# The weights of three of seven up-projection products, moved by 64 bytes inside longer ring buffers

## The chip, the cores and the metric

The kernel runs on one core of a Trainium2 chip. The metric is the device time of one execution in microseconds (us); the number compared is the median of several runs. The profiled execution is one further run, and all rows of the profile come from it.

## What is computed

One layer of a hybrid decoder trunk on 512 tokens with 2048 channels, in float32: a norm, a combined input projection, three groups of mixing heads, an output projection, a gated feed-forward part and a last norm. The reference, cut:

```python
def reference(x, norm1_w, w_in, ..., final_norm_w):
    for l in range(DEPTH):                                    # DEPTH = 1
        h = rmsnorm(x, norm1_w[l])
        u_pool, q, k, v, z, a, bt, xr, gr = jnp.split(h @ w_in[l], cuts, axis=-1)
        y_pool = pool_mixer(u_pool, ...)
        y_gdn = gated_deltanet(q, k, v, z, a, bt, ...)
        y_lru = rglru_mixer(xr, gr, ...)
        mixed = jnp.concatenate([y_pool, y_gdn, y_lru], axis=-1)
        x = x + mixed @ w_out[l]
        x = x + conv_ffn(rmsnorm(x, norm2_w[l]), ffn_up[l], ffn_conv_w[l], ffn_down[l])
    return rmsnorm(x, final_norm_w)

def conv_ffn(h, w_up, conv_w, w_down):
    gate, val = jnp.split(h @ w_up, 2, axis=-1)               # 2048 -> 2 x 6144
    gate = causal_dwconv(gate, conv_w)
    return (jax.nn.gelu(gate) * val) @ w_down                 # 6144 -> 2048
```

## The kernel before

**Products.** Every large product is made of three matmuls on TensorE (PE). Both operands are split into a high and a low part of a reduced float32 format (fp32r): ScalarE (ACT) casts the high part, VectorE (DVE) subtracts it to get the low one, and PE adds hi x hi, hi x low and low x hi into one PSUM bank. The weights are the stationary operand, tiles of 128 x 128 out of a buffer of 128 x 1024, and are loaded anew for each matmul; the tokens are the moving operand. PE and the DMA queue of SyncE (SP) run in the order in which the code is written. In the first part DVE, ACT and GpSimd (POOL) are ordered by the compiler's scheduler, from the up projection on also by the code.

**Stages.** `in_phase` makes 40 units of the input projection, with the heads' work put between them as coroutines (`gdn_gates`, `gdn_front`, `gdn_pair`, `lru_front` and others); then come the output projection, the up projection (class `UpProjection`), the down projection and the last norm.

**The weights' ring.** A weight block is loaded into a `raw` buffer and split into `hi` and `lo`. There are four buffers of each (`NW`), used in turn through the whole kernel, of 4096 bytes a partition: `prep` at L180 for the input and output projections, `split` at L1165 for the up projection, `w_split` at L972 for the down projection.

**The up projection.** It is computed by a scheme with seven products in place of eight (L1123 and following). Weights and tokens are cut in two; for each of the 48 column groups j seven combinations of weight blocks are multiplied with seven forms of the tokens. Three forms are plain blocks (`BLOCKS`: a11, a12, a22), four are sums of blocks (`SUMS`: s1 to s4). A product (`product`, L1180) has 8 steps of three matmuls with 256 moving columns. `ACT_FORM` says which form each product takes:

```python
    ACT_FORM = {"b22": "s4", "b11": "a11", "t3": "s3", "t1": "s1", "t2": "s2", "b21": "a12", "t4": "a22"}
```

A slot is one product; a column group starts seven slots after the one before, so that each stretch of seven slots (a round) holds one of each kind. The weights' combinations are made in place: after a split, POOL issues a DMA that adds the next block into the same `raw` buffer (L1178). Blocks are loaded 7 slots ahead (`LEAD`) and split 3 slots ahead (`LAG`).

**Where the tiles lie.** A tile's place in a partition follows from the pools' order and sizes. The parameters take 1220 bytes, the constants 2048, and what follows lies in steps of 2048 and 4096 bytes. In the built program all `hi` and `lo` buffers and all tiles of the pool `acts` begin 96 bytes into a block of 128 bytes. In `acts` are the split tokens of all projections, the plain blocks (`fa`, `fb`), and the sums' tiles for p = 6 and 7 (`split_sums`, L824: the branch after `p < HK - 2`). The sums' tiles for p = 0 to 5 are in the pool `ffn` and begin 32 bytes into a block of 128. The index p is also the product's step. In the trace the names are `fs` for sums, `fa` and `fb` for plain blocks, `hi_b`, `hi_t`, `lo_b`, `lo_t` for the up projection's weights, and `ps_x`, `ps_y`, `ps_z` for its PSUM banks; the bank does not tell the form, the moving operand's name does.

**Gates and constants.** `cst` in the pool `const` holds four 128 x 128 constants: identity, upper triangle, mask and ones. `softplus` (L138) is used twice in the input phase, for the recurrent block's constants (`spl`, in `lru_consts`) and for the decay gates (`spg`, in `gdn_gates`), on four small scratch tiles each in the pool `g1`. Two short matmuls `ps_g` (L460, L461) take its result `g`; in PE's order the transposes of k and q and what follows of the first heads stand right behind them.

Of the kernel before, what the change touches and what calls it, by code (L numbers as in the profile page):

```python
# [8 lines left out]
F32 = mybir.dt.float32  # L9
F32R = mybir.dt.float32r  # L10
# [8 lines left out]
P = 128  # L19
# [11 lines left out]
NW = 4  # L31
# [4 lines left out]
COL = {}  # L36
# [31 lines left out]
DOWN_GAP = 1.2  # L68
ND = 4
NWARM = 14  # L70
# [9 lines left out]
class Body:  # L80
# [3 lines left out]
    def __init__(self, tc, io):  # L84
        self.tc, self.nc, self.io = tc, tc.nc, io
        self.now, self.cos, self.polling = 0.0, [], False


# [48 lines left out]

    def softplus(self, pool, out, x, n, tag, sign=1.0):  # L138

        nc = self.nc  # L140
        ab = pool.tile([P, n], F32, tag=f"{tag}a", name=f"{tag}_abs")
        u = pool.tile([P, n], F32, tag=f"{tag}u", name=f"{tag}_u")
        s = pool.tile([P, n], F32, tag=f"{tag}s", name=f"{tag}_s")
        z = pool.tile([P, n], F32, tag=f"{tag}z", name=f"{tag}_z")
        nc.vector.tensor_scalar(ab, x, -1.0, None, op0=ALU.mult)
        nc.vector.tensor_tensor(out=u, in0=ab, in1=x, op=ALU.min)
        nc.scalar.activation(u, u, AF.Exp)
        nc.vector.tensor_scalar(s, u, 2.0, None, op0=ALU.add)
        nc.vector.reciprocal(s, s)
        nc.vector.tensor_tensor(out=s, in0=s, in1=u, op=ALU.mult)  # L150
        nc.vector.tensor_tensor(out=z, in0=s, in1=s, op=ALU.mult)
        nc.vector.memset(u, 1.0 / 17.0)
        for k in (15, 13, 11, 9, 7, 5, 3, 1):
            nc.vector.tensor_tensor(out=u, in0=u, in1=z, op=ALU.mult)
            nc.vector.tensor_scalar(u, u, 1.0 / k, None, op0=ALU.add)
        nc.vector.tensor_tensor(out=u, in0=u, in1=s, op=ALU.mult)
        nc.vector.tensor_scalar(ab, x, sign, 0.0, op0=ALU.mult, op1=ALU.max)
        nc.vector.scalar_tensor_tensor(out=out, in0=u, scalar=2.0, in1=ab, op0=ALU.mult, op1=ALU.add)
# [20 lines left out]

    def prep(self, src, name, pre="w"):  # L180

        nc = self.nc
        raw = self.wp.tile([P, 1024], F32, tag="raw", name=f"raw_{name}", bufs=3)
        nc.sync.dma_start(out=raw, in_=src)
        pool, n = (self.wp, NW) if pre == "w" else (self.wd, ND)
        hi = pool.tile([P, 1024], F32R, tag=pre + "hi", name=f"hi_{name}", bufs=n)
        lo = pool.tile([P, 1024], F32R, tag=pre + "lo", name=f"lo_{name}", bufs=n)
        nc.scalar.copy(out=hi, in_=raw)  # L188
        nc.vector.tensor_tensor(out=lo, in0=raw, in1=hi.bitcast(F32), op=ALU.subtract)  # L189
        return hi, lo  # L190
# [53 lines left out]
    def run(self):  # L244
        tc, nc, io = self.tc, self.nc, self.io
        with ExitStack() as ctx:
# [9 lines left out]
            self.prmt = cp.tile([P, NPRM], F32, name="prmt")  # L256
            cst = cp.tile([P, 4, P], F32, name="cst")
            self.ident, self.upper, self.mask, self.ones = (cst[:, i, :] for i in range(4))
            self.cst = cst
            self.in_phase()  # L260
# [16 lines left out]
    def in_phase(self):  # L277
        tc, nc, io = self.tc, self.nc, self.io
        with ExitStack() as ctx:
# [20 lines left out]

            n1 = g1.tile([P, KT], F32, name="n1")

            warm = self.tmp("warm")
# [25 lines left out]
            for kt in range(KT):  # L329
# [5 lines left out]
                if kt == 12:  # L335
                    nc.sync.dma_start(out=self.cst, in_=io["cst"])
                    nc.sync.dma_start(out=self.prmt, in_=io["prm"])
# [91 lines left out]
    def gdn_gates(self, ssum, psab):  # L429
# [24 lines left out]
        nc.scalar.activation(ea, hb[:, 0:1, :], AF.Exp)  # L454
        self.softplus(g1, f2(g), f2(x), n, "spg")
        nc.vector.scalar_tensor_tensor(out=g, in0=g, scalar=-1.0, in1=ea.broadcast_to([P, NC, H]),
# [243 lines left out]
    def lru_consts(self):  # L700
        nc, g1 = self.nc, self.g1
        n = NB
        sp = g1.tile([P, n], F32, name="lsp")
        self.softplus(g1, sp, self.prmt[:, COL["lam"]:COL["lam"] + n], n, "spl", sign=-1.0)
        self.sc, self.nsc = g1.tile([P, n], F32, name="lsc"), g1.tile([P, n], F32, name="lnsc")
        nc.vector.tensor_scalar(self.sc, sp, -8.0, None, op0=ALU.mult)
        nc.vector.tensor_scalar(self.nsc, sp, 8.0, None, op0=ALU.mult)
# [77 lines left out]
    def out_phase(self):  # L785
        tc, nc, io = self.tc, self.nc, self.io
        with ExitStack() as ctx:
# [184 lines left out]
            def w_split(c, k):  # L972
                hi, lo = (self.wp.tile([P, 1024], F32R, tag=t, name=f"{t}_d{c}_{k}", bufs=NW) for t in ("whi", "wlo"))
                self.parts(raws.pop((c, k)), hi, lo)
                wd.setdefault(c, []).append((hi, lo))
# [147 lines left out]
class UpProjection:  # L1123
# [41 lines left out]
    def split(self, n):  # L1165

        nc, wp = self.nc, self.b.wp
        while self.n_split < min(n, len(self.slots)):
            _, j, f = self.slots[self.n_split]
            self.n_split += 1  # L1170
            raw = self.raw[j, self.CHAIN[f][0]]
            hi = wp.tile([P, 1024], F32R, tag="whi", name=f"hi_{f}_{j}", bufs=NW)
            lo = wp.tile([P, 1024], F32R, tag="wlo", name=f"lo_{f}_{j}", bufs=NW)
            nc.scalar.copy(out=hi, in_=raw)  # L1174
# [85 lines left out]
def _layout(inputs):  # L1260
# [28 lines left out]
    up = i[None, :] >= i[:, None]  # L1289
    r["cst"] = c(np.stack([np.eye(P), up, np.where(up, 0.0, -1e30), np.ones((P, P))]).astype(np.float32)  # L1290
                 .transpose(1, 0, 2))
# [23 lines left out]
```

## Time and profile before

| | us |
|---|---|
| median of 3 runs | 2236.95 |
| range of the runs | 2236.02 to 2238.54 |
| the profiled execution's own time | 2237.1 |
| its span, first to last instruction | 2235.3 |
| first 105 us of it: PE busy | 99.2 |
| input phase and output projection, 105 to 751 us: PE busy | 633.2 |
| up projection, 775 to 1691 us: PE busy | 914.5 |
| down projection, 1702 to 2210 us: PE busy | 508.0 |
| end, 2210 to 2235 us: PE busy | 11.8 |

The up projection's first products run from 740 us on. Rows that begin with a window A:B give its length, then each engine's busy time and number of instructions (PE, PE's weight loads, DVE, ACT, POOL; an engine without instructions is left out), the granted TensorE clock as a share of the full one, the DMA engines' busy share, and GB/s. Rows of the chain and the timeline give start and duration. Rows of groups give busy time and mean ns of one, then the engine's idle time before them and what ended it. Matmuls overlap: one begins while the one before it still drains, so the pace of a stream is the distance between starts, not the duration. Rows of waits give total, number and the longest.

### The profile page before, as it was taken

The numbers are of one execution on the slowest core, as the hardware profiler recorded it, in microseconds if no ns is written. First come the engines' busy times: TensorE is split into PE (matmuls) and PEld (weight loads), VectorE is DVE, ScalarE is ACT, GpSimd is POOL, SyncE is SP. The second block draws the span as 40 slices with busy tenths as digits, with TensorE's granted clock in tenths as the row PEclk, the third lists the DMA queues.
The fourth block names the chain that finished last, engine by engine and source line by source line (L and its number), as shares of the span: only waits on it lengthen the run. The fifth ranks groups of instructions, "written<-read, shape, count | busy, mean of one in ns | idle before, by whom it ended". The sixth has DMA issues, their size and how long they took to land.

```text
span 2235.3 us, 35469 instructions
## 1 busy us (share of the span) xinstructions
PE 2199.9 (98%) x13998; PEld 1991.0 (89%) x13998; DVE 1517.4 (68%) x2340; ACT 944.6 (42%) x1371; POOL 437.6 (20%) x531
## 2 busy tenths in 40 slices
PE   9999999999999999999999999999999999999997
PEld 6878878888888999999999999999998888888887
DVE  8756657664544776667676677676667777777776
ACT  6646455433433544444444444444443222222223
POOL 4270730810122111111111111111110000000004
PEclk9999999999999999999999999999999999999998
DMA  6222222223533788888889888888885333333333
GB/s 199 83 95 66 88 85 81 91 86 112 192 123 117 164 209 207 200 203 198 195 204 209 199 202 196 198 204 207 210 197 189 130 120 126 123 113 123 113 127 100
DMA packets 109208, 340.01 MB, mean 152 GB/s; under 512 B 12720, under 2 KB 19120, under 8 KB 109040
## 3 DMA queue, kind: packets, MB, share of 16 engines
q1 hardware_dynamic: 78576, 229.72, 30.1%
q0 software_dynamic: 30464, 108.02, 26.6%
q8 instruction: 110, 1.80, 0.3%
q14 instruction: 58, 0.48, 0.1%
HBM read 314.36 MB, written 23.33 MB: 151 GB/s over the span
## 4 chain that ended last, share of the span: by engine, by line
PE 85%; POOL 5%; DVE 4%; issue 2%; ACT 2%; DMA 2%; SPq 0%; POOLq 0%; ACTq 0%; DVEq 0%
PE ps_y L1193 17%; PE ps_x L1193 12%; PE ps_z L1193 11%; PE ps_d L203 7%; PE ps_d L201 7%; PE ps_d L202 7%; PE ps_u L201 3%; PE ps_u L202 3%; PE ps_u L203 3%; PE ps_o L202 3%; PE ps_o L201 3%; PE ps_o L203 3%; POOL tm L581 2%; POOL tl L583 2%; DVE lo_in L189 1%
## 5 line engine op out<-in xcount | busy, mean ns | idle before, releaser
L1010 DVE TENSOR_TENSOR accd<-accd,ps_d 128x512 f32<-128x512 f32 x368 | 250.0, 685 | 125.1 <-PE ps_d L203 125.0
L201 PE MATMUL ps_d<-gh,whi_d 128*128 128x512 f32 x736 | 286.3, 389 | 0.0
L202 PE MATMUL ps_d<-gl,whi_d 128*128 128x512 f32 x736 | 286.3, 389 | 0.0
L203 PE MATMUL ps_d<-gh,wlo_d 128*128 128x512 f32 x736 | 286.3, 389 | 0.0
L1193 PE MATMUL ps_y<-fs,hi_t 128*128 128x256 f32 x1536 | 269.8, 278 | 1.8 <-DVE e L1219 1.8
L274 ACT CAST whi_d<-raw_d 128x1024 fp32r<-128x1024 f32 x96 | 100.8, 1053 | 371.7 <-PE ps_d L202 345.5
L1175 DVE TENSOR_TENSOR lo_t<-ra,hi_t 128x1024 fp32r<-128x1024 f32 x144 | 176.0, 1223 | 112.9 <-ACT hi_t L1174 112.8
L201 PE MATMUL ps_u<-xh,hi_in 128*128 128x512 f32 x608 | 246.4, 405 | 0.0
L203 PE MATMUL ps_u<-xh,lo_in 128*128 128x512 f32 x608 | 238.7, 393 | 0.0
L202 PE MATMUL ps_u<-xl,hi_in 128*128 128x512 f32 x608 | 238.1, 392 | 0.0
L1178 POOL DMA_DIRECT2D ra<-in_w_up x144 | 126.2, 876 | 556.8 <-DVE lo_t L1175 457.5
L1193 PEld LDWEIGHTS ps_y<-fs,hi_t 128*128 128x128 f32 x1536 | 233.1, 188 | 2.2 <-ACT hi_b L1174 1.7
L1193 PE MATMUL ps_y<-fs,lo_t 128*128 128x256 f32 x768 | 213.1, 278 | 0.0
L1174 ACT CAST hi_t<-ra 128x1024 fp32r<-128x1024 f32 x144 | 151.3, 1051 | 69.8 <-PE ps_y L1193 43.5
L202 PEld LDWEIGHTS ps_d<-gl,whi_d 128*128 128x128 f32 x736 | 138.1, 188 | 28.8
L203 PEld LDWEIGHTS ps_d<-gh,wlo_d 128*128 128x128 f32 x736 | 138.1, 188 | 28.6
L201 PEld LDWEIGHTS ps_d<-gh,whi_d 128*128 128x128 f32 x736 | 138.1, 188 | 28.6
L189 DVE TENSOR_TENSOR lo_in<-raw_in,hi_in 128x1024 fp32r<-128x1024 f32 x80 | 104.4, 1306 | 78.0 <-ACT hi_in L188 77.4
L1193 PEld LDWEIGHTS ps_y<-fs,lo_t 128*128 128x128 f32 x768 | 144.4, 188 | 0.0
L1193 PE MATMUL ps_y<-fb,hi_t 128*128 128x256 f32 x768 | 140.1, 283 | 1.2 <-DVE e L1223 1.2
L1193 PE MATMUL ps_x<-fb,hi_b 128*128 128x256 f32 x768 | 140.1, 283 | 0.0
L1193 PE MATMUL ps_x<-fa,hi_b 128*128 128x256 f32 x768 | 140.0, 283 | 0.0
(357 smaller groups left out, 5104.7 us busy)
## 6 DMA issues: line engine op xcount, KB each, us to landing
ra<-in_w_up POOLq DMA_DIRECT2D x144, 512.0 KB, 7.7
raw_d<-in_w_down SPq DMA_DIRECT2D x96, 512.0 KB, 4.2
raw_in<-in_w_in SPq DMA_DIRECT2D x80, 512.0 KB, 3.7
ra<-in_w_up SPq DMA_DIRECT2D x48, 512.0 KB, 7.0
rc<-in_w_up SPq DMA_DIRECT2D x48, 512.0 KB, 6.5
rb<-in_w_up SPq DMA_DIRECT2D x48, 512.0 KB, 7.2
rb<-in_w_up POOLq DMA_DIRECT2D x48, 512.0 KB, 7.2
raw_o<-in_w_out SPq DMA_DIRECT2D x32, 512.0 KB, 3.7
```

The lines of the kernel that those rows point to most:

```text
L189: nc.vector.tensor_tensor(out=lo, in0=raw, in1=hi.bitcast(F32), op=ALU.subtract)
L201: nc.tensor.matmul(ps, hi[:, sl], a, start=start, stop=False)
L202: nc.tensor.matmul(ps, hi[:, sl], b, start=False, stop=False)
L203: nc.tensor.matmul(ps, lo[:, sl], a, start=False, stop=stop)
L274: self.nc.scalar.copy(out=hi, in_=x)
L581: nc.gpsimd.tensor_tensor(out=t, in0=bc(ll[:, j, j + 1:32], j + 1), in1=tl[:, j:j + 1, 0:j + 1].broadcast_to([32, m, j + 1]), op=ALU.mult)
L583: nc.gpsimd.tensor_tensor(out=tl[:, j + 1:32, 0:j + 1], in0=tl[:, j + 1:32, 0:j + 1], in1=t, op=ALU.subtract)
L1010: nc.vector.tensor_tensor(out=acc[d], in0=acc[d], in1=ps, op=ALU.add)
L1174: nc.scalar.copy(out=hi, in_=raw)
L1175: nc.vector.tensor_tensor(out=lo, in0=raw, in1=hi.bitcast(F32), op=ALU.subtract)
L1178: nc.gpsimd.dma_start(out=raw, in_=self.block(j, self.NEXT[f]), accum_op=ALU.add)
L1193: mm = lambda w, x, s, e: nc.tensor.matmul(ps, w[:, sl], x, start=s, stop=e, skip_group_check=True)
```

## The change

The ring's buffers become 1040 words (4160 bytes) long in place of 1024, one tag for each, taken in turn by a counter; a weight block fills 1024 words of its buffer, from the first word or from the 17th. Because 4160 bytes are 32.5 blocks of 128, the `hi` buffers begin 96 bytes into such a block and the `lo` buffers 32. `weight_parts` chooses the offset (0 or 64 bytes) so that hi and lo lie at 96 for all products but three, and at 32 for the products with plain blocks (b11, b21, t4). To make room, the upper triangle and the mask move into a pool of the input phase (two loads in place of one), and softplus's scratch becomes one tile of the ring of temporaries for each use.

```diff
-    def softplus(self, pool, out, x, n, tag, sign=1.0):
+    def softplus(self, out, x, n, tag, sign=1.0):
...
-        ab = pool.tile([P, n], F32, tag=f"{tag}a", name=f"{tag}_abs")
-        u = pool.tile([P, n], F32, tag=f"{tag}u", name=f"{tag}_u")
-        s = pool.tile([P, n], F32, tag=f"{tag}s", name=f"{tag}_s")
-        z = pool.tile([P, n], F32, tag=f"{tag}z", name=f"{tag}_z")
+        scr = self.tmp(f"{tag}_scratch", [P, 4, n])
+        ab, u, s, z = (scr[:, i, :] for i in range(4))
...
-    def prep(self, src, name, pre="w"):
+    def weight_parts(self, name, other=False):
+        i = self.n_ring % NW
+        self.n_ring += 1
+        t = [self.wp.tile([P, 1040], F32R, tag=f"w{p}{i}", name=f"{p}_{name}", bufs=1) for p in ("hi", "lo")]
+        o = [16 * ((k + other) % 2) for k in range(2)]
+        return [t[k][:, o[k]:o[k] + 1024] for k in range(2)]
+
+    def prep(self, src, name):
...
-        pool, n = (self.wp, NW) if pre == "w" else (self.wd, ND)
-        hi = pool.tile([P, 1024], F32R, tag=pre + "hi", name=f"hi_{name}", bufs=n)
-        lo = pool.tile([P, 1024], F32R, tag=pre + "lo", name=f"lo_{name}", bufs=n)
+        hi, lo = self.weight_parts(name)
...
-            cst = cp.tile([P, 4, P], F32, name="cst")
-            self.ident, self.upper, self.mask, self.ones = (cst[:, i, :] for i in range(4))
-            self.cst = cst
+            self.cst = cp.tile([P, 2, P], F32, name="cst")
+            self.ident, self.ones = (self.cst[:, i, :] for i in range(2))
...
+            cst2 = g1.tile([P, 2, P], F32, name="cst2")
+            self.upper, self.mask = (cst2[:, i, :] for i in range(2))
...
-                    nc.sync.dma_start(out=self.cst, in_=io["cst"])
+                    nc.sync.dma_start(out=self.cst, in_=io["cst"][:, 0:2])
+                    nc.sync.dma_start(out=cst2, in_=io["cst"][:, 2:4])
...
-                hi, lo = (self.wp.tile([P, 1024], F32R, tag=t, name=f"{t}_d{c}_{k}", bufs=NW) for t in ("whi", "wlo"))
+                hi, lo = self.weight_parts(f"d{c}_{k}")
...
-            hi = wp.tile([P, 1024], F32R, tag="whi", name=f"hi_{f}_{j}", bufs=NW)
-            lo = wp.tile([P, 1024], F32R, tag="wlo", name=f"lo_{f}_{j}", bufs=NW)
+            hi, lo = self.b.weight_parts(f"{f}_{j}", other=self.ACT_FORM[f] in BLOCKS)
```

On PE and POOL the instructions stand in the same order as before, over the whole kernel, and from the output projection on so do those of DVE, ACT and SP. The scheduler's order changes on DVE and ACT in the first units of the input projection. DVE around the gates, before: `spg_u` and `spg_abs` are softplus's scratch, `x_q` and `cv_q` the second q head's evacuation and convolution, `lo_in` the low part of the next unit's weights, `g` the gates, `G` their sums out of PSUM.

```order
L413 TENSOR_TENSOR x_q_711<-ps_u_650,rstd1b 128x512
L156 TENSOR_TENSOR spg_u<-spg_u,spg_s 128x24
L158 SCALAR_TENSOR_TENSOR g<-spg_u,spg_abs 128x24
L189 TENSOR_TENSOR lo_in_1_708<-raw_in_1_705,hi_in_1_707 128x1024
L456 SCALAR_TENSOR_TENSOR g<-g,ea 128x24
L425 SCALAR_TENSOR_TENSOR cv_q_713<-x_q_711,prmt,cv_q_713 128x511
L464 COPY G<-ps_g 128x48
```

The same place of the changed kernel, whose line numbers are 7 higher here (L156 and L158 of before are L154 and L156 of the changed kernel, and L189 is L194):

```order
L420 TENSOR_TENSOR x_q_707<-ps_u_646,rstd1b 128x512
L153 TENSOR_SCALAR spg_scratch<-spg_scratch 128x24
L154 TENSOR_TENSOR spg_scratch<-spg_scratch 128x24
L194 TENSOR_TENSOR lo_in_1_704<-raw_in_1_701,hi_in_1_703 128x1024
L156 SCALAR_TENSOR_TENSOR g<-spg_scratch 128x24
L432 SCALAR_TENSOR_TENSOR cv_q_709<-x_q_707,prmt,cv_q_709 128x511
L463 SCALAR_TENSOR_TENSOR g<-g,ea 128x24
L432 SCALAR_TENSOR_TENSOR cv_q_709<-x_q_707,prmt,cv_q_709 128x510
L471 COPY G<-ps_g 128x48
```

The last steps to g have moved behind the low part, and one convolution step of cv_q stands ahead of the last of them.

SP's queue near the end of the first two units, before: `xraw` are the token tiles, `prmt` the parameters, `raw_in` the third unit's weights.

```order
L313 DMA xraw_368<-in_xT 128x512
L336 DMA cst<-in_cst 128x512
L337 DMA prmt<-in_prm 128x305
L313 DMA xraw_387<-in_xT 128x512
L184 DMA raw_in_0_420<-in_w_in 128x1024
```

In the changed kernel, where the upper triangle and the mask have a transfer of their own:

```order
L319 DMA xraw_369<-in_xT 128x512
L342 DMA cst<-in_cst 128x256
L343 DMA cst_101<-in_cst 128x256
L344 DMA prmt<-in_prm 128x305
L319 DMA xraw_389<-in_xT 128x512
L191 DMA raw_in_0_422<-in_w_in 128x1024
```

One issue stands ahead of the parameters, of the last token tile and of the weights that follow.

More of the change, by code (lines that the diff above doesn't have):

```diff
@@ L68 @@
 DOWN_GAP = 1.2
-ND = 4
 NWARM = 14
@@ L86, in __init__ @@
         self.now, self.cos, self.polling = 0.0, [], False
+        self.n_ring = 0
     def spawn(self, gen):
@@ L454, in gdn_gates @@
         nc.scalar.activation(ea, hb[:, 0:1, :], AF.Exp)
-        self.softplus(g1, f2(g), f2(x), n, "spg")
+        self.softplus(f2(g), f2(x), n, "spg")
         nc.vector.scalar_tensor_tensor(out=g, in0=g, scalar=-1.0, in1=ea.broadcast_to([P, NC, H]),
@@ L703, in lru_consts @@
         sp = g1.tile([P, n], F32, name="lsp")
-        self.softplus(g1, sp, self.prmt[:, COL["lam"]:COL["lam"] + n], n, "spl", sign=-1.0)
+        self.softplus(sp, self.prmt[:, COL["lam"]:COL["lam"] + n], n, "spl", sign=-1.0)
         self.sc, self.nsc = g1.tile([P, n], F32, name="lsc"), g1.tile([P, n], F32, name="lnsc")
@@ L1165, in split @@
     def split(self, n):
-        nc, wp = self.nc, self.b.wp
+        nc = self.nc
         while self.n_split < min(n, len(self.slots)):
@@ L1289, in _layout @@
     up = i[None, :] >= i[:, None]
-    r["cst"] = c(np.stack([np.eye(P), up, np.where(up, 0.0, -1e30), np.ones((P, P))]).astype(np.float32)
+    r["cst"] = c(np.stack([np.eye(P), np.ones((P, P)), up, np.where(up, 0.0, -1e30)]).astype(np.float32)
                  .transpose(1, 0, 2))
```

## The prediction

> **What bounds the kernel now.** I read the page's first part and the windows by stage first, then what TensorE (PE) waits for.
>
> ```profile
> PE 2199.9 (98%) x13998; PEld 1991.0 (89%) x13998; DVE 1517.4 (68%) x2340; ACT 944.6 (42%) x1371; POOL 437.6 (20%) x531
> 775.00:1691.00 916.00, 914.50 (x7805) 914.15 (x7804) 639.18 (x795) 434.46 (x560) 160.22 (x183) 1.00 0.85 201
> 1702.00:2210.00 508.00, 508.00 (x2315) 423.77 (x2315) 376.12 (x526) 131.19 (x164) 12.06 (x17) 1.00 0.37 120
> PE ps_yt L118 <- ACT hi_in L188: 5.8, 1, 5.8
> PE ps_y L1193 <- DVE e L1219: 1.8, 2, 1.5
> ```
>
> PE is busy for 98% of the span. In the up projection (775 to 1691 us here) it works 914.5 of 916 us at a granted clock of 1.00, and its weight loads fill the same 914 us. The two waits quoted are the longest of all and the longest in the up projection: 1.8 us in a stage of over 900. So in this stage a shorter PE instruction is a shorter kernel, and nothing else is. In the down projection PE is busy without a gap too, but its operands keep their places.
>
> Next, one round of the up projection in the chain that ended last: seven products of 24 matmuls, one row each.
>
> ```profile
> 1003.25 2.88 PE ps_y L1193 x24
> 1006.13 2.76 PE ps_z L1193 x24
> 1008.89 2.88 PE ps_x L1193 x24
> 1011.77 2.76 PE ps_y L1193 x24
> 1014.53 2.88 PE ps_x L1193 x24
> 1017.41 2.77 PE ps_y L1193 x24
> 1020.17 2.76 PE ps_z L1193 x24
> ```
>
> In order these are t4, b22, b11, t2, b21, t3, t1. Each has 24 matmuls of the same size, and still t4, b11 and b21, the three whose moving operand is a plain block (fa, fb), take 2.88 us, and the four whose moving operand is a sum (fs) take 2.76. The timeline of PE across the end of t1 and the start of t4 shows where that sits (start, duration):
>
> ```profile
> 1001.70 0.39 PE L1193 MATMUL ps_z<-fs,hi_t 128*128 128x256 f32 x2
> 1001.93 0.28 PE L1193 MATMUL ps_z<-fs,lo_t 128*128 128x256 f32 x1
> 1002.04 0.39 PE L1193 MATMUL ps_z<-fs,hi_t 128*128 128x256 f32 x2
> 1002.27 0.28 PE L1193 MATMUL ps_z<-fs,lo_t 128*128 128x256 f32 x1
> 1002.38 0.39 PE L1193 MATMUL ps_z<-fs,hi_t 128*128 128x256 f32 x2
> 1002.62 0.28 PE L1193 MATMUL ps_z<-fs,lo_t 128*128 128x256 f32 x1
> 1002.73 0.40 PE L1193 MATMUL ps_z<-fs,hi_t 128*128 128x256 f32 x2
> 1002.97 0.28 PE L1193 MATMUL ps_z<-fs,lo_t 128*128 128x256 f32 x1
> 1003.09 0.40 PE L1193 MATMUL ps_y<-fb,hi_t 128*128 128x256 f32 x2
> 1003.32 0.28 PE L1193 MATMUL ps_y<-fb,lo_t 128*128 128x256 f32 x1
> 1003.44 0.40 PE L1193 MATMUL ps_y<-fb,hi_t 128*128 128x256 f32 x2
> ```
>
> Count from one hi row to the next: a step is two matmuls on hi and one on lo. The steps are 0.34 and 0.34 us, then 0.35 and 0.36, then 0.35 in the block product, whose mean step is 2.88 / 8 = 0.36. The two slow steps inside t1 are its last two, p = 6 and 7. Those tiles are the sums kept in the acts pool, 96 bytes into a block of 128 like every weight tile; the sums p = 0 to 5 lie in the ffn pool, 32 bytes into it. The product, the weights and the kind of operand are the same, and the step changes with the place alone: **moving operand and weights 64 bytes apart, 0.34 us; at the same place, 0.36**. The sum agrees: 6 x 0.34 + 2 x 0.36 = 2.76. The blocks all lie at 96, so all of their steps are slow.
>
> **The change part by part.** *The weights of the three block products* go from 96 to 32 in the block; their moving operands stay at 96. That is the same distance of 64 bytes with the two operands' places exchanged, and this exchange is what no row of before shows. Ends: nothing, if only the moving operand's place counts (its steps stay at 0.36), and all eight steps at 0.34, which saves 8 x 0.02 = 0.16 us a product. I take the second, less its start: a block product follows a sum product, which ends in slow steps, and the row at 1002.38 shows one in-between step of 0.35 at a change of place. One step's worth of loss, and rows that are rounded to 0.01, leave 0.13 to 0.14; I take 0.135, that is 2.745 us a product. There are 3 x 48 = 144 such products: 144 x 0.135 = **19.4 us less** (0.12 to 0.16 each: 17.3 to 23.0).
>
> *Sums p = 6 and 7, and every 512-column matmul*, keep both operands at 96: no change.
>
> *The split that writes the weights* gets outputs 64 bytes further on, on ScalarE (ACT) and VectorE (DVE). Its rows in the up projection, with the transfer that refills the buffer:
>
> ```profile
> L1174 ACT CAST hi_t<-ra 128x1024 fp32r<-128x1024 f32 x139 | 146.1, 1051 | 69.1 <-PE ps_y L1193 43.5 <-DMA ra<-in_w_up 21.3 <-PE ps_z L1193 4.2
> L1175 DVE TENSOR_TENSOR lo_t<-ra,hi_t 128x1024 fp32r<-128x1024 f32 x139 | 169.9, 1223 | 110.9 <-ACT hi_t L1174 110.8
> L189 DVE TENSOR_TENSOR lo_in<-raw_in,hi_in 128x1024 fp32r<-128x1024 f32 x80 | 104.4, 1306 | 78.0 <-ACT hi_in L188 77.4
> L1178 POOL DMA_DIRECT2D ra<-in_w_up x137 | 120.0, 876 | 531.9 <-DVE lo_t L1175 451.0 <-DVE lo_b L1175 41.1 <-DMA ra<-in_w_up 24.8
> ra<-in_w_up POOLq DMA_DIRECT2D x137, 512.0 KB, 7.7
> ```
>
> The cast waits mostly for PE to free a ring buffer (43.5 + 4.2 of 69.1 us), so it runs as early as the ring lets it, three products or some 8 us ahead of its use. What a write 64 bytes further on costs no row shows; the nearest are the same low part at two lines, 1.22 and 1.31 us, so -0.08 to +0.08 us each. The lead hides either: cost nothing. Without it, 0.08 us on 144 products would be 12 us.
>
> *What is late next, with PE faster:* the transfers. A refill of ra takes cast 1.05, low part 1.22, issue 0.88 and a median of 7.7 to land, at most 10.85 us in all, and has four slots for it: the round's seven rows make 19.69 us, a slot 2.81, four 11.25 before and 4 x 2.755 = 11.0 after. The margin shrinks from 0.40 to 0.17 us, and more of ACT's waits will be for the DMA. They eat into the 8 us of lead, and a chain has only three such refills before it starts afresh, so they reach PE at nothing. Mean traffic goes from 201 to 201 x 916 / 897 = 205 GB/s, with DMA engines busy 0.87 instead of 0.85.
>
> *The ring* still has four hi and four lo buffers in the same order, and no wait is added. *Softplus's scratch and the constants* change the order on DVE ahead of the decay gates:
>
> ```profile
> 68.26 1.22 DVE L189 TENSOR_TENSOR lo_in<-raw_in,hi_in 128x1024 fp32r<-128x1024 f32 x1
> 69.39 0.18 DVE L456 SCALAR_TENSOR_TENSOR g<-g,ea 128x24 f32<-128x24 f32 x1
> 69.49 0.74 DVE L425 SCALAR_TENSOR_TENSOR cv_q<-x_q,prmt,cv_q 128x511 f32<-128x511 f32 x1
> 69.86 0.29 PE L460 MATMUL ps_g<-g,cst 128*128 128x24 f32 x2
> 29.90 0.43 SPq L336 DMA_DIRECT2D cst<-in_cst  x1
> 35.48 0.72 ACT L238 ACTIVATE xh<-xraw,n 128x512 fp32r<-128x512 f32 x1 [1.70 <-DMA xraw<-in_xT]
> 41.50 0.59 ACT L438 COPY abT<-psab 128x512 f32<-128x512 f32 x1 [1.93 <-PE psab L339]
> ```
>
> Before, g is done at 69.57 and PE takes it up at 69.86: 0.29 us to spare. Now one more small step of softplus (0.18) and a convolution step (0.74) stand between that lo_in and g: 0.92 - 0.29 = 0.6 us of new waiting at ps_g. Queued behind it in PE's fixed order are the transposes of k and q and the next unit, and all that hangs on the gates, so I charge it in full: **0.6 us more** (0 to 0.9). The second constant load is one more issue on SP's queue, 0.43 us, ahead of prmt, the last tile of x and the next weights; that tile's split starts at 35.48, and PE's last step on it, eight matmuls of about 0.23 us, ends with psab at 41.5, so it begins near 39.6, three microseconds after the split: hidden; without that cover, 0.4.
>
> *Sum.* The profiled execution took 2237.1 us (span 2235.3, and 1.8 around it): 2237.1 - 19.4 + 0.6 = 2218.3. The median of the runs shown, 2236.95, lies 0.15 below that execution: **2218.2 us**. With the ends of the terms: 2214 to 2221.
>
> **A rule that speaks against it.** The Trainium skill, "SBUF — State Buffer", section "Who interferes with whom", gives PE two independent read ports of SBUF, one for the moving operand and one for the weight load, and has PE waiting on no one. By it the place of the weights cannot matter, and the sum would be 2237.6. The trace has a step that changes with the place of the moving operand (0.34 and 0.36), which that rule doesn't explain, but every weight tile of before lies at 96, so the rule is not refuted for the weights.
>
> **The rivals.** *The moving operand's own place decides* (at 32 fast, at 96 slow). For it: of the two places only the moving one varies in this trace. Against it: what else is at work during a matmul is the load of the next weights, which is as long as the stage (914.15 us), and a place mod 128 that costs one stream time by itself would need a reason that a pair doesn't. Then nothing is saved: 2237.0 + 0.6 = 2237.6.
>
> *Slower: places other than the two pairs seen cost more.* Of the fp32r matmuls, only the mixers' small products (ps_l and ps_p, both operands at 0) and the a/b columns (psab, 96 against 64) lie otherwise:
>
> ```profile
> L203 PE MATMUL ps_d<-gh,wlo_d 128*128 128x512 f32 x736 | 286.3, 389 | 0.0
> L201 PE MATMUL ps_l<-xch,w 128*128 128x512 f32 x12 | 4.8, 396 | 0.0
> L201 PE MATMUL ps_u<-xh,hi_in 128*128 128x512 f32 x608 | 246.4, 405 | 0.0
> L339 PE MATMUL psab<-xl,wab 128*128 128x512 f32 x16 | 6.8, 423 | 0.8 <-DVE xl L239 0.8
> ```
>
> ps_l is 7 ns longer than ps_d, though ps_d has the slow pair. If 32 for the weights were such a place, 48 x 3 x 24 = 3456 block matmuls would each pay up to 7 ns: 2237.6 + 24 = 2262 at most, and it decides against the change from the first nanosecond, once a block product passes 2.88 us. Against it: ps_l comes in sixes between the matmuls of ps_u, which have the slow pair and a mean as long (405), so the stretch may be dear rather than the place; psab holds the kernel's first matmuls and their waits.
>
> *Half of it:* the pair repeats over more than 128 bytes. Ring buffers are now 4160 bytes apart, so neighbours would then differ, and only half of the block products gain: 2237.6 - 9.7 = 2228.
>
> **How the numbers follow.** Forecast 0.78, the moving operand alone 0.12, slower 0.05, half 0.05. The predicted time is the forecast's, 2218.2. The range runs from 2212, a little below the low end of the terms for what the sum products may gain at their first step, to 2228, the half: 0.83 of the chance. A measurement of this kernel tells about 0.2% (4.5 us) from no change: faster 0.83 (forecast and half), within it 0.12, slower 0.05.
>
> **What would show it.** Right: in the chain the rows of t4, b11 and b21 fall from 2.88 to about 2.74, steps of 0.34 us in them; sums stay at 2.76; ps_d stays at 389 ns; the up projection is 19 us shorter and every other stage as long as before; a wait of about 0.6 us at ps_g. Wrong: block rows at 2.88 (the moving operand decides), above it (slower), or alternating between two lengths from ring buffer to ring buffer (half); or PE waits at L1193 for hi or lo after the first rounds, which would mean the transfers don't keep up.

## The result, and the profile after

| | before | after |
|---|---|---|
| median, us | 2237.07 (2236.02 to 2238.54, 4 runs) | 2249.61 (2248.97 to 2251.96, 4 runs) |
| ratio, 95% interval | | 1.0057 [1.004, 1.0075] |
| profiled execution, us | 2237.1 (span 2235.3) | 2251.96 (span 2250.2) |
| forecast | | 2218.2 (2212 to 2228) |

The kernel became slower by 12.5 us, where 19 us less had been forecast. All runs in this document had a granted clock of 0.99 or more but one, of the last control kernel, which took 3295.28 us at 0.62 and is in no ratio. The page of the changed kernel has PE even busier than before:

```profile
PE 2218.4 (99%) x13998; PEld 1987.8 (88%) x13998; DVE 1518.2 (67%) x2340; ACT 945.6 (42%) x1371; POOL 435.9 (19%) x531
```

There are as many matmuls (13998) in 18.5 us more of PE, so it is not waiting that has grown: matmuls have become longer. Two marks in the chain that ended last show in which stage. The marks are a product of the up projection's first rounds, the one that is issued just after the second norm's last step, and the first matmul of the down projection. Before:

```profile
763.04 3.08 PE ps_y L1193 x24
1691.32 0.23 PE ps_d L201
```

After:

```profile
770.88 2.99 PE ps_y L1199 x24
1695.53 0.23 PE ps_d L206
```

Up to the first mark 7.8 us were lost. Between the marks 924.65 us stand against 928.28: the up projection gained 3.6 us. From the second mark to the end of the span it is 554.7 against 544.0: 10.7 lost. 7.8 - 3.6 + 10.7 = 14.9 us, which is the whole difference of the two spans.

**The 512-column matmuls**, of which the forecast said that they would not change, are the loss. Groups of instructions by form, after:

```profile
L208 PE MATMUL ps_d<-gh,lo_d 128*128 128x512 f32 x736 | 290.5, 395 | 0.0
L206 PE MATMUL ps_u<-xh,hi_in 128*128 128x512 f32 x608 | 247.8, 408 | 0.0
```

Their rows of before have 389 and 405 ns, so they are 6 and 3 ns longer; the two other rows of ps_d have 394 and 393 in place of 389. A matmul's duration overlaps its neighbours', so what one really costs is the distance from start to start. The windows view of a stretch in which PE is never idle gives it: the length through the count. Before, first a stretch of the output projection, then one of the down projection (its instructions on ps_d alone):

```profile
570.00:740.00 170.00, 170.00 (x751) 1.00 0.46 149
1730.00:1900.00 170.00, 170.00 (x752) 1.00 0.38 124
```

After, the same two:

```profile
570.00:740.00 170.00, 170.00 (x733) 1.00 0.44 147
1730.00:1900.00 170.00, 170.00 (x735) 1.00 0.36 118
```

At the same granted clock of 1.00, 170 us hold 733 and 735 matmuls in place of 751 and 752: 231.9 and 231.3 ns each in place of 226.4 and 226.1. On the 2208 matmuls of ps_d 5.2 ns are 11.5 us (10.7 were measured), on the 768 of ps_o 5.5 ns are 4.2 us. What is left of the first 7.8, some 3.6 us, lies ahead of the output projection, and the weights' places explain little of it. Two kernels below (the ring alone, and the changed kernel with the sums' order) have their weights at the same places up to there, and their first mark stands at 768.31 and 768.13, 5.3 and 5.1 us later than before's. So some 2.6 us are this one execution's own; it is also the longest of its four, 2.35 above their median. The input projection's ps_u, although its matmuls are longer too, costs about 1 us. PE also waits in that stage (it is busy for 510.64 of the 524 us from 43 to 567 before, for 514.63 after), which fits longer matmuls that fill time that was idle.

**The up projection.** One round of the chain that ended last, after; in order b21, t3, t1, t4, b22, b11, t2:

```profile
1001.35 2.83 PE ps_x L1199 x24
1004.18 2.80 PE ps_y L1199 x24
1006.98 2.78 PE ps_z L1199 x24
1009.75 2.83 PE ps_y L1199 x24
1012.58 2.76 PE ps_z L1199 x24
1015.34 2.83 PE ps_x L1199 x24
1018.17 2.76 PE ps_y L1199 x24
```

The three block products (b21, t4, b11) went from 2.88 to 2.83 us, not to 2.745; two of the four sum products, which were to stay at 2.76, went to 2.80 and 2.78. 144 x 0.05 = 7.2 us gained, less 48 x (0.04 + 0.02) = 2.9 us: 4.3, near the 3.6 measured. In the next round t3 is back at 2.76, and b22 goes to 2.80:

```profile
1023.75 2.76 PE ps_y L1199 x24
1032.12 2.80 PE ps_z L1199 x24
```

The sums b22, t2 and t3 go on like this from round to round: a round has seven products and neighbouring ring buffers differ, so a product of one kind finds the other kind of buffer in the next round. Alternating rows were the sign that the prediction named for "half of it"; they came, but in the sums, not in the blocks.

**The wait at ps_g**, among PE's waits, came with the new order of the gates, as forecast and a little smaller (waited for, us in total, times, longest):

```profile
PE ps_g L467 <- DVE g L463: 0.4, 1, 0.4
```

### The profile page after: what moved, and what is told of

The parts are those of the page before. It is cut to its first block, busy times and chain, and to the rows that moved or that the text cites. A ratio compares the mean times of both kernels' runs of the same rounds, so it can differ in the third digit from the quotient of the medians.

```text
span 2250.2 us, 35466 instructions
## 1 busy us (share of the span) xinstructions
PE 2218.4 (99%) x13998; PEld 1987.8 (88%) x13998; DVE 1518.2 (67%) x2340; ACT 945.6 (42%) x1371; POOL 435.9 (19%) x531
## 4 chain that ended last, share of the span: by engine, by line
PE 85%; POOL 5%; DVE 4%; issue 2%; DMA 2%; ACT 1%; SPq 0%; POOLq 0%; ACTq 0%; DVEq 0%
PE ps_y L1199 17%; PE ps_x L1199 12%; PE ps_z L1199 11%; PE ps_d L208 8%; PE ps_d L207 8%; PE ps_d L206 8%; PE ps_u L207 3%; PE ps_u L206 3%; PE ps_u L208 3%; PE ps_o L208 3%; PE ps_o L207 3%; PE ps_o L206 3%; POOL tm L588 2%; POOL tl L590 2%; DMA rb<-in_w_up 1%
## 5 line engine op out<-in xcount | busy, mean ns | idle before, releaser
L208 PE MATMUL ps_d<-gh,lo_d 128*128 128x512 f32 x736 | 290.5, 395 | 0.0
L207 PE MATMUL ps_d<-gl,hi_d 128*128 128x512 f32 x736 | 289.8, 394 | 0.0
L206 PE MATMUL ps_d<-gh,hi_d 128*128 128x512 f32 x736 | 289.0, 393 | 0.0
L278 ACT CAST hi_d<-raw_d 128x1024 fp32r<-128x1024 f32 x96 | 100.3, 1052 | 383.9 <-PE ps_d L207 363.3
L1181 DVE TENSOR_TENSOR lo_t<-ra,hi_t 128x1024 fp32r<-128x1024 f32 x144 | 176.0, 1223 | 119.1 <-ACT hi_t L1180 116.2
L1180 ACT CAST hi_t<-ra 128x1024 fp32r<-128x1024 f32 x144 | 151.4, 1052 | 77.2 <-PE ps_y L1199 39.5
L207 PEld LDWEIGHTS ps_d<-gl,hi_d 128*128 128x128 f32 x736 | 138.1, 188 | 32.9
L206 PEld LDWEIGHTS ps_d<-gh,hi_d 128*128 128x128 f32 x736 | 138.5, 188 | 32.4
L208 PEld LDWEIGHTS ps_d<-gh,lo_d 128*128 128x128 f32 x736 | 138.1, 188 | 31.8
L194 DVE TENSOR_TENSOR lo_in<-raw_in,hi_in 128x1024 fp32r<-128x1024 f32 x80 | 105.1, 1315 | 78.3 <-ACT hi_in L193 77.8
L208 PEld LDWEIGHTS ps_u<-xh,lo_in 128*128 128x128 f32 x608 | 114.6, 189 | 26.4
```

Source lines behind the costliest of these rows:

```text
L206: nc.tensor.matmul(ps, hi[:, sl], a, start=start, stop=False)
L207: nc.tensor.matmul(ps, hi[:, sl], b, start=False, stop=False)
L208: nc.tensor.matmul(ps, lo[:, sl], a, start=False, stop=stop)
L278: self.nc.scalar.copy(out=hi, in_=x)
```

## The experiments

The theory that came of the two traces (P in the expectations): what counts is how far the weights lie from the moving operand **modulo 256 bytes**, not 128. By the order and sizes of the tiles, before, the weights lie at 224 of 256, the split tokens, the gated activations and the blocks too, the sums p = 0 to 5 at 160. Call weights less moving operand, modulo 256, the difference: it was 0 for every 512-column matmul and every block, and 64 for the sums. A ring buffer of 4160 bytes is 16.25 times 256, so in the changed kernel the parts lie in turn at 224, 96, 96, 224, and the 512-column matmuls have differences of 0 and 128 mixed. The letters in the expectations name the theories; what each said is told where its run is read.

### The constants alone, the ring alone

The first kernel keeps the changed softplus and constants, with the ring of before:

```diff
-        t = [self.wp.tile([P, 1040], F32R, tag=f"w{p}{i}", name=f"{p}_{name}", bufs=1) for p in ("hi", "lo")]
-        o = [16 * ((k + other) % 2) for k in range(2)]
+        t = [self.wp.tile([P, 1024], F32R, tag=f"w{p}{i}", name=f"{p}_{name}", bufs=1) for p in ("hi", "lo")]
+        o = [0, 0]
```

> The changed kernel with ring buffers of 4096 bytes again, no offset for the plain blocks: only the constants and softplus's scratch are changed. Theory P (the places of weights and moving operand, taken over 256 bytes, set the pace of the matmul stream): the input, output, up and down stages are as long as before (524, 174, 950, 501 us), plus some 0.4 us at the gates: 2237.5 us. Rival S (the scheduler's new order or the moved constants cost the time): 2245 to 2250 us, with the loss in the input stage.

Measured: 2236.1 us (10 runs), 0.9999 [0.9989, 1.0008] of before. The constants' part of the change costs nothing that can be told, as P has it, and rival S falls.

The second has the longer ring, and all weights at the same place in the block of 128:

```diff
-            hi, lo = self.b.weight_parts(f"{f}_{j}", other=self.ACT_FORM[f] in BLOCKS)
+            hi, lo = self.b.weight_parts(f"{f}_{j}", other=False)
```

> The changed kernel with no offset for the plain blocks: all weights 96 bytes into a block of 128, in buffers 4160 bytes apart, so that neighbouring buffers differ by 128 bytes within 256. Theory P: the 512-column stages lose as in the changed kernel (down 511 us, output 178 us, ps_d at 394 ns), and the block products are between 2.83 and 2.88 us: 2250 to 2257 us. Rival O (the offset of the block products disturbs its surroundings, the ring's length is nothing): 2237 us, ps_d at 389 ns.

Measured: 2260.3 us (2259.66 to 2262.53), 1.0106 [1.0091, 1.0121]. The longer ring by itself costs 23 us, and the blocks' other half of 128 bytes brings 11 of them back. The 2260.3 lies 3 us above P's range, which counted nothing for the sums. Three rows of its chain (b21, t3, t1):

```profile
1001.54 2.86 PE ps_x L1199 x24
1004.39 2.78 PE ps_y L1199 x24
1007.18 2.78 PE ps_z L1199 x24
```

The blocks are at 2.86, and the sums, whose weights have merely moved by 128 bytes in half of the parts, are dearer than 2.76 (t3 here at 2.78, in the round after it at 2.86). That the other half of the block was the harm (rival O) falls.

### A ring with one place for all

Hi and lo of one buffer in one tile of 8448 bytes, 33 times 256: each part lies where it lay before, modulo 256, and the blocks' weights 64 bytes further on. To make room one small tile of the mixers has one buffer.

```diff
-        t = [self.wp.tile([P, 1040], F32R, tag=f"w{p}{i}", name=f"{p}_{name}", bufs=1) for p in ("hi", "lo")]
-        o = [16 * ((k + other) % 2) for k in range(2)]
-        return [t[k][:, o[k]:o[k] + 1024] for k in range(2)]
+        t = self.wp.tile([P, 2112], F32R, tag=f"w{i}", name=f"w_{name}", bufs=1)
+        return [t[:, 1024 * k + 16 * other:1024 * k + 16 * other + 1024] for k in range(2)]
...
-        small = lambda tag, nm: self.tp.tile([P, P], F32, tag=tag, name=nm, bufs=3 if tag == "st" else 2)
+        small = lambda tag, nm: self.tp.tile([P, P], F32, tag=tag, name=nm, bufs={"st": 3, "r": 1}.get(tag, 2))
```

> One buffer of 8448 bytes (33 x 256) per ring slot holds hi and lo, 4096 bytes apart; the plain blocks' weights still lie 64 bytes further on. Every weight tile is now at one place within 256 bytes (224, or 32 for the blocks); slots differ by 256 within 512. (The ring of small tiles r in the head scans has one buffer in place of two, for room: up to some us in the input stage.) Theory P, period 256: the 512-column stages return to before (down 501, output 174 us, ps_d at 389 ns), block products at 2.83 us or less: 2230 to 2236 us, or about 2218 if they settle at 2.72. Rival L (the places matter over 512 bytes or more): down stays at 508 to 512 us, 2245 us or more.

Measured: 2230.89 us (2228.55 to 2233.44, 10 runs), 0.9976 [0.9966, 0.9985]. The same two stretches, windows view:

```profile
570.00:740.00 170.00, 170.00 (x752) 1.00 0.43 149
1730.00:1900.00 170.00, 170.00 (x751) 1.00 0.36 123
```

With the difference back at 0 the 512-column matmuls are back at 226 ns, in a ring that is still longer than before. So the 4160 bytes did harm by the places they give. Neighbouring slots here differ by 256 bytes within 512, and that costs the 512-column matmuls nothing: rival L falls, and the time is inside P's 2230 to 2236 us. This kernel beats both. In its profiled execution the first mark stands at 767.37 us, 4.3 later than before's. I had put that to the small tile, but a later kernel with the same buffers (in the last pair below) has it at 763.67. Over the input projection, 43 to 567 us, the windows give this execution a granted clock of 0.98 and that later one 0.99; whether that is all of it is left open.

A round of its chain (t1, t4, b22, b11, t2, b21, t3) shows what the theory did not say:

```profile
1002.49 2.76 PE ps_z L1198 x24
1005.25 2.74 PE ps_y L1198 x24
1007.99 2.83 PE ps_z L1198 x24
1010.82 2.83 PE ps_x L1198 x24
1013.65 2.76 PE ps_y L1198 x24
1016.41 2.74 PE ps_x L1198 x24
1019.14 2.83 PE ps_y L1198 x24
```

All but two steps of each sum product have the difference 64 here, and there are two paces at it: t4 and b21 run at 2.74, which is what was forecast, b11 at 2.83; the sums t1 and t2 at 2.76, b22 and t3 at 2.83. From 900 us to the stage's last round every round of this trace repeats these times.

### Is the pace that in which a product is entered?

In before, a sum product's last two steps (p = 6 and 7, at the difference 0) take 0.36 us in place of 0.34, and the next product comes in behind them. Theory E: a product keeps the pace of the steps behind which it starts. (The rows above already speak against it for the sums: t3 starts behind b21, which runs at 2.74, and takes 2.83; t1 starts behind t3 and takes 2.76.) To test it on the blocks, the changed kernel has the sums' steps 6 and 7 issued first:

```diff
-        for kt in range(HK):
+        steps = range(HK) if self.ACT_FORM[f] in BLOCKS else [6, 7, 0, 1, 2, 3, 4, 5]
+        for n, kt in enumerate(steps):
...
-            st, en = first and kt == 0, kt == HK - 1
+            st, en = first and n == 0, n == HK - 1
```

> The changed kernel, with the steps of the four sum products in the order 6, 7, 0 to 5, so that the two steps whose operands lie at the same place come first and a block product follows a fast step. Theory E (a stream keeps the pace with which it starts; the block products start behind slow steps and keep 117.8 ns a matmul): block products at 2.72 to 2.75 us in place of 2.83, the up stage some 12 to 16 us shorter, 2235 to 2238 us; the other stages as in the changed kernel. Rival F (the exchanged places have a pace of their own, 117.8 ns, whatever comes before): block products at 2.83, 2248 to 2251 us.

Measured: 2244.44 us (2244.01 to 2244.62), 1.0033 [1.002, 1.0046]: 5 us better than the change, and 6 us above the upper end of what was expected. Its chain, from t1 on (then t4, b22, b11):

```profile
1003.11 2.85 PE ps_z L1200 x24
1005.96 2.75 PE ps_y L1200 x24
1008.71 2.84 PE ps_z L1200 x24
1011.54 2.72 PE ps_x L1200 x24
```

The blocks came to 2.72 to 2.75, the time that E gives, with nothing changed in them, so rival F falls: the exchanged places have no pace of their own. But the sums, that hold the same matmuls in another order, went from 2.76 to 2.80 up to 2.84 and 2.85 us in this round and gave most of it back. And E's reason is not there. PE across the end of b22 and the start of b11, of the timeline the rows on hi alone, so that each stands for one step:

```profile
1010.67 0.40 PE L1200 MATMUL ps_z<-fs,hi_b 128*128 128x256 f32 x2
1011.02 0.40 PE L1200 MATMUL ps_z<-fs,hi_b 128*128 128x256 f32 x2
1011.38 0.39 PE L1200 MATMUL ps_x<-fa,hi_b 128*128 128x256 f32 x2
1011.72 0.39 PE L1200 MATMUL ps_x<-fa,hi_b 128*128 128x256 f32 x2
```

The block starts behind steps of 0.35 and 0.36 us, and runs at 0.34 from its first step on.

### Moving one operand's pool at a time

Three kernels have the ring of before (4096 bytes) and the constants of the first experiment, and shift whole pools by padding tiles whose sum is a multiple of 256 bytes. The acts pool 192 bytes on, so that every product of the up projection, and every 512-column matmul, has the difference 64:

```diff
             self.wp = pool("wts", bufs=1)
+            pool("pad0", bufs=1).tile([P, 48], F32, name="pad0")
             self.ap_ = pool("acts", bufs=1)
+            pool("pad1", bufs=1).tile([P, 16], F32, name="pad1")
```

> The kernel of the run with constants and softplus alone (ring of 4096 bytes, 2236.1 us), with unused pads of 192 bytes before and 64 bytes after the pool of split tokens: every moving operand of the large products lies at 160 within 256 bytes, every weight at 224, a difference of 64 bytes throughout, the one that sums 0 to 5 have in the kernel before. Theory D (the difference weights less moving, over 256 bytes, sets the pace, and a stream that keeps one difference settles): all up products at 2.72 to 2.74 us, up stage about 917 us, the 512-column matmuls at about 220 ns in place of 226.7 (down 486, output 169, input 512 us): 2170 to 2180 us. Rival M (the moving operand's own place): the same here. Rival N (512-column matmuls have a floor at 226.7 ns whatever the places): only the up stage gains, 2203 us.

Measured: 2262.17 us, 1.0095 [1.0071, 1.0119], a median that lies 59 us above the highest of the three expectations. The 10 runs fall into two groups, eight at 2261.58 to 2263.78 and two at 2241.08 and 2243.17, at granted clocks of 0.994 to 0.996 in both. In the profiled execution, of the slower group, every product of the chain has the slower pace, and the stretch of the down projection has 731 matmuls, 232.6 ns each, so that rival N's floor of 226.7 falls as well:

```profile
1000.74 2.83 PE ps_y L1201 x24
1003.56 2.83 PE ps_x L1201 x24
```

```profile
1730.00:1900.00 170.00, 170.00 (x731) 1.00 0.35 115
```

So the same program with the same addresses has more than one time, which no theory here expected. That the faster runs are those in which more products run at 2.72 is argued, since no trace of such a run was taken.

The weights' pool 64 bytes on, the moving operands where they were (differences 64 for blocks and 512 columns, 128 for the sums p = 0 to 5):

```diff
+            pool("pad0", bufs=1).tile([P, 16], F32, name="pad0")
             self.wp = pool("wts", bufs=1)
+            pool("pad1", bufs=1).tile([P, 48], F32, name="pad1")
             self.ap_ = pool("acts", bufs=1)
```

> The same with the pads of 64 bytes before and 192 after the pool of weights: every weight at 32 within 256 bytes, the split tokens at 224 as before (difference 64), sums 0 to 5 still at 160 (difference 128). Theory D: the 512-column stages, the block products and the sums' steps 6 and 7 as in the run before this one (down 486 us, blocks 2.72 to 2.74), the sums' steps 0 to 5 slower than 113.3 ns. Rival M: nothing changes against before but a loss or none at the sums: down 501 us, block products 2.88.

Measured: 2253.19 us (2252.83 to 2253.5), 1.007 [1.0055, 1.0085]. Its chain (t1, t4) and its stretch on ps_d:

```profile
1005.43 2.85 PE ps_z L1201 x24
1008.29 2.72 PE ps_y L1201 x24
```

```profile
1730.00:1900.00 170.00, 170.00 (x730) 1.00 0.36 118
```

Every block is at 2.72. The sum's last two steps ahead of it, from the acts pool, have the difference 64, but in the timeline they take 0.36 and 0.35 us (from 1007.41 to 1008.12), so no fast step stands ahead of the block here either. No moving operand has moved, and the blocks have gone from 2.88 to 2.72 and the sums from 2.76 to 2.85: that the moving operand's own place decides (theory M) falls. And 512 columns at the difference 64 take 170 / 730 = 232.9 ns: what is best for 256 columns is not for 512 (theory D, one best difference for all, falls). The run before this one has other places for both operands and the same difference, and with it nearly the same pace (731 in 170 us): that speaks for the difference and against either place by itself.

The weights' pool 128 bytes on. It asks whether the mixture in the changed kernel is dear because it alternates (theory A) or because 128 is itself a dear difference (rival B):

```diff
+            pool("pad0", bufs=1).tile([P, 32], F32, name="pad0")
             self.wp = pool("wts", bufs=1)
+            pool("pad1", bufs=1).tile([P, 32], F32, name="pad1")
             self.ap_ = pool("acts", bufs=1)
```

> Pads of 128 bytes before and after the pool of weights: every weight at 96 within 256 bytes, split tokens at 224, so that the 512-column matmuls and the block products have a fixed difference of 128 bytes. Theory A (what the longer ring costs comes of buffers that alternate between two differences, so that the stream never settles): the 512-column matmuls settle as before, 226.7 ns, down 501 us. Rival B (a difference of 128 is itself slow): 231 to 233 ns, down about 511 us, without alternation.

Measured: 2264.35 us (2262.95 to 2268.16), 1.0124 [1.0107, 1.0141]. The stretch on ps_d, and two products of the chain, a block (b21) and a sum (t3, here at the difference 192):

```profile
1730.00:1900.00 170.00, 170.00 (x730) 1.00 0.35 115
```

```profile
1002.35 2.85 PE ps_x L1201 x24
1005.20 2.82 PE ps_y L1201 x24
```

At a fixed difference of 128 it is 232.9 ns, more than the mixture's 231.3: the difference itself is dear, alternation isn't needed (B).

### The best ring with the other order, and the other order alone

The ring of 8448 bytes with the order of the fourth experiment, and as its control the ring of before with that order.

> The longer ring of two periods (8448 bytes, every buffer at the same place over 256 bytes), and the steps p = 6, 7 of the sums' products issued ahead of p = 0 to 5. Theory E (the pace of a 256-column stream is that in which it enters, and every product now enters through a fast or a settled place): blocks 2.72 to 2.74 us, sums 2.76 to 2.78 us, the 512-column stages as in the kernel before (down some 500 us), the stage of the way in still 4 to 5 us longer by its one small buffer: 2208 to 2218 us. Rival G (the sums give back what the blocks gain, as they did with the order alone on the changed kernel, 2.78 to 2.85 us each): 2224 to 2232 us, no better than the ring of two periods alone.

> The kernel before with nothing but the order of the sums' steps changed (p = 6, 7 first) and the two constants in their new pool. Blocks have both operands at one place, which has run at one settled pace of 2.87 us whatever went before: theory E expects no change of the blocks, the sums within 0.02 us of before, 2234 to 2239 us. Rival: the order by itself is worth what it brought on the changed kernel, 5 us: 2229 to 2233 us.

Measured: 2233.8 us (2231.14 to 2237.05, 11 runs), 0.9983 [0.9974, 0.9992], and for the control 2236.43, 0.9995 [0.9986, 1.0004] (12 runs, 11 of them at 2235.48 to 2237.05). Two products of the chain of the first (t4, b22), then two of the control's (t4, b22):

```profile
1002.52 2.83 PE ps_y L1199 x24
1005.35 2.78 PE ps_z L1199 x24
```

```profile
1002.93 2.86 PE ps_y L1200 x24
1005.79 2.78 PE ps_z L1200 x24
```

Theory E, which gave 2208 to 2218 us, falls: a sum's 2.76 to 2.78 us are two steps of 0.36 and then six of about 0.34, so each block now does start behind fast steps, and runs at 2.83 all the same, where t4 and b21 ran at 2.74 with the old order. Some sums gain (b22 from 2.83 to 2.78) while those blocks lose 0.09. That is the reverse of what rival G names, and the time is 1.8 us above G's range, but the kernel is no better than the ring of 8448 alone, as G said. The order alone is worth nothing.

All that was measured at a granted clock of 1.00, with the difference that each kind of matmul has (of the sums, that of the steps p = 0 to 5):

| kernel | 512 columns: difference, ns | blocks: difference, us | sums: difference, us | us |
|---|---|---|---|---|
| before | 0, 226 | 0, 2.88 | 64, 2.76 | 2237 |
| ring alone | 0 and 128, 231 | 0 and 128, 2.86 | 64 and 192, 2.78 to 2.86 | 2260 |
| after | 0 and 128, 231 | 64 and 192, 2.83 | 64 and 192, 2.76 to 2.80 | 2250 |
| before, sums' order | 0, 226 | 0, 2.86 | 64, 2.76 and 2.78 | 2236 |
| after, sums' order | the same as after | 2.72 to 2.75 | 2.78 to 2.85 | 2244 |
| ring of 8448 | 0, 226 | 64, 2.74 and 2.83 | 64, 2.76 and 2.83 | 2231 |
| ring of 8448, sums' order | 0, 226 | 64, 2.83 | 64, 2.76 and 2.78 | 2234 |
| acts moved | 64, 233 | 64, 2.83 | 64, 2.83 | 2262 or 2242 |
| weights moved by 64 | 64, 233 | 64, 2.72 | 128, 2.85 | 2253 |
| weights moved by 128 | 128, 233 | 128, 2.85 | 192, 2.82 | 2264 |

## Why the prediction was wrong

**The step that failed** is "*Sums p = 6 and 7, and every 512-column matmul*, keep both operands at 96: no change." It took the place modulo 128 bytes. Modulo 128 nothing moved; modulo 256 half of the weight parts moved by 128, and 512-column matmuls went from 226 to 231 ns. The ring of 8448 bytes shows it from one side (places back, 226 ns) and the weights moved by 128 from the other (233 ns with the ring of before). That alone is some 10.7 us in the down projection and 4.2 in the output projection, on a term that was put at nothing.

The period was in the prediction, as the rival called half of it. It priced the period in the wrong place: only in the blocks, half of which would not gain. In fact +64 and +192 gave blocks the same 2.83, and the cost fell on matmuls that the change was not about. The rule that I had read from one pair of rows (apart is fast, together is slow) was a rule for 256 columns; for 512, together is fast and the differences of 64 and 128 are slow, and the rows of before could not show that, since all their 512-column matmuls had the difference 0, apart from the 16 of psab.

**The block term was mis-sized.** 0.135 us a product was charged, 0.05 came: 2.83 in place of 2.745. The pair does get faster when it is taken apart, and 2.72 exists, but at 64 a stream holds either 2.72 or 2.83, and in the changed kernel nearly all blocks hold the slower. Which one a stream falls into is **left open**. The pace of the steps ahead doesn't tell: blocks have held 0.34 us a step behind steps of 0.35 and 0.36, and 2.83 us a product behind steps of 0.34. It is no accident of a single product either, since each kind repeats its time round after round, yet one program has shown two times in different runs.

**The moving operand's own place** was given 0.12. It falls: moving only the weights took 0.16 us off each block. The Trainium skill, "SBUF — State Buffer", section "Who interferes with whom", gives PE two independent read ports. From that the prediction had drawn that the weights' place cannot matter; for these fp32r matmuls the measurement says that it does.

**Slower** had the right sign and 0.05, by another mechanism: that the blocks themselves would pass 2.88. They did not; they are the one part that gained.

**The rest held, but for one wait.** The wait at ps_g came, 0.4 us for 0.6, and can't be told in the time (the constants alone: 0.9999). The splits' output place cost nothing: cast and low part take 1052 and 1223 ns, as before (1051 and 1223). More of the casts' waits are for the DMA, as was said (37.4 us of 77.2). Groups by form:

```profile
L1180 ACT CAST hi_t<-ra 128x1024 fp32r<-128x1024 f32 x144 | 151.4, 1052 | 77.2 <-PE ps_y L1199 39.5 <-DMA ra<-in_w_up 37.4
L1181 DVE TENSOR_TENSOR lo_t<-ra,hi_t 128x1024 fp32r<-128x1024 f32 x144 | 176.0, 1223 | 119.1 <-ACT hi_t L1180 116.2 <-PE ps_y L1199 2.8
```

In the steady rounds they don't reach PE. In the last round one does: PE's longest wait on its line, 1.2 us, is there, where before had 1.8 - 1.5 = 0.3. The chain that ended last goes back from it, by DVE's e and a split, to a transfer into rb, which took 8.11 us in place of 7.24. First the wait after, then the transfer before and after:

```profile
PE ps_y L1199 <- DVE e L1225: 2.1, 2, 1.2
1669.76 7.24 DMA rb<-in_w_up
1673.15 8.11 DMA rb<-in_w_up
```

So in this execution the transfers' term, put at nothing, cost some 0.9 us, which covers the 0.7 between the 4.3 us by products and the 3.6 by marks.

The sum by measured terms: 2237.1 - 7.2 (blocks) + 2.9 (sums) + 10.7 (down) + 4.2 (output projection) + 0.4 (ps_g) = 2248.1, against a median of 2249.61 and 2251.96 for the profiled execution. Of the 3.9 us that are missing against the latter, some 2.6 are that execution's own (by the first mark), 0.7 the up projection's (4.3 less 3.6), and the rest lies in the input projection, beside ps_g.

## What to carry to other kernels

When a buffer's length changes, list the place of every operand that uses it, modulo more than the period you believe in, and price every kind of matmul that reads it, above all the ones the change isn't for. A pace read from one shape (256 columns) is no rule for another (512 columns). And where rows show two paces, look for what holds a stream in one before you charge the better one to all.

## What was not expected of the hardware

- The cost of an fp32r matmul depends on weights' place less moving operand's place, modulo 256 bytes in these kernels, and the best difference depends on the length: 512 columns take 226 ns at 0 and 233 at 64 and at 128; 256 columns take 2.88 / 24 = 120 ns at 0, 2.85 / 24 = 119 at 128, and 2.72 / 24 = 113 or 2.83 / 24 = 118 at 64.
- At the difference 64 two paces, 2.72 and 2.83 us a product, each last through whole products, in one kernel side by side (2.74 and 2.83 in the ring of 8448). One kernel's runs fall into two groups 20 us apart, at the same places.
- Within one execution the pace repeats: in the ring of 8448, b11 took 2.83 us and t4 and b21 2.74 in round after round, and in the changed kernel the sums b22, t2 and t3 alternated between 2.76 and 2.80 with the buffers. What sets the pace, no run here shows.
